# Chunk attention: a mask tile for the far scores, a joint maximum by a seeded minimum, one exponential a block, reciprocals once a step

## The chip, the cores and the metric

The kernel runs on one core of a Trainium2 chip. The metric is the device time of one execution in microseconds (us). Engines: PE is TensorE (matrix products and transposes), DVE is VectorE, ACT is ScalarE, POOL is GpSimd, and SP issues most of the DMAs. Each engine works through its own list of instructions in order, and semaphores make it wait for the others.

## The reference, cut to what matters

A trunk of two layers over 1024 positions of width 1024. The first is a mixer of two recurrent kinds, the second is softmax attention over chunks of 64 positions; each is followed by an MLP and a gated embedding. The change lies in the attention alone:

```python
q = rmsnorm(qkv[:, :, 0], q_g) * (C_HEAD_DIM ** -0.5)      # 16 heads of 64
k = rmsnorm(qkv[:, :, 1], k_g)
rel = jnp.arange(CHUNK)[:, None] + pad - jnp.arange(band)[None, :]   # pad = 8*64, band = 9*64
bias = rel_bias[:, jnp.clip(rel, -C_MAX_REL, C_MAX_REL) + C_MAX_REL]  # C_MAX_REL = 256
...
s = jnp.einsum('bqhd,bkhd->bhqk', q_c, k_b) + bias
s = jnp.where(valid, s, -jnp.inf)
prob = jax.nn.softmax(s, -1)
return jnp.einsum('bhqk,bkhd->bqhd', prob, v_b)
```

Each chunk of 64 queries sees its own chunk and the eight before it. The bias of a head is one constant for all distances from 256 up, and softmax doesn't change when a constant is taken from a whole row: so the kernel takes that constant off, and the far keys need no bias at all.

## The kernel before, in words

The second layer's attention works in 16 steps: 8 pairs of heads, and for each pair two halves of 512 positions. `attn_in` makes q, k and v of a half-step by matrix products (tile `dps` in the profile, from the weights `wq`), `attn_norm` transposes q and k (`dps<-ident,qk`) and scales them into `F` and `Ql`, `attn_block` does the attention, and `attn_sums` scales and stores the result of a finished step.

A block is one head and one tile of 128 queries, numbered m = 0 to 7 over the sequence; there are 16 x 8 = 128 blocks. Its key tiles fall in two groups. The near ones (up to 3 tiles of 128 keys: m-2, m-1, m) get a bias tile `toep`, which also masks. The far ones (up to 2: m-4 and m-3) get none, only a corner that is masked. Blocks with m of 0 to 2 have no far tile (48 blocks), m of 3 has one (16 blocks), m of 4 to 7 have two (64 blocks). For each block:

- PE makes the near scores in the PSUM tile `sn` (two buffers) and the far scores in `sf` (one buffer).
- DVE adds the bias to the near scores, writes them to `pb` and takes their maximum (L2024, an operation and the read of its accumulator). For the far ones it writes the masked corner into `sf` (L2031), takes their maximum (L2032) and forms the negated joint maximum in `mx` (L2033; without far keys L2036).
- ACT takes the exponential of the far scores from `sf` (L2034) and of the near ones in `pb` (L2037), each with the sum of its row.
- DVE adds the two sums (L2039) and takes the reciprocal into `rl` (L2041). In the last two steps ACT also scales `pb` by it (L2043).

Two blocks make a job. PE transposes `pb` into `pt` (two PSUM buffers), ACT and DVE split it into two parts in `ptile` (L352 a rounded copy, L353 the remainder), and PE multiplies it with the values into `po`. Two lanes of jobs run beside each other, with the projections of a later step as filling for PE. At the end of each of the first 14 steps `attn_sums` transposes the eight columns of `rl` on PE, stores them, loads them back as rows, and POOL scales the result.

The order of the work comes from two places: `run` takes the next piece from the lanes by planned times, with the delays of a table, and the tile framework's scheduler then puts the instructions of each engine in order by its own estimates. So an edit in `attn_block` can also move instructions around it.

Of the kernel before, what the change touches and what calls it, by code (L numbers as in the profile page):

```python
# [8 lines left out]
F32 = mybir.dt.float32  # L9
F32R = mybir.dt.float32r  # L10
I32 = mybir.dt.int32
AF = mybir.ActivationFunctionType
ALU = mybir.AluOpType
AX = mybir.AxisListType
# [3 lines left out]
P = 128  # L18
# [3 lines left out]
HB = 512  # L22
NT = T // P
C = 128
NEG = -1.0e30
# [87 lines left out]
class Trunk:  # L113
# [393 lines left out]
    def layer0_in(self):  # L507
        nc, tc, a = self.nc, self.tc, self.a
        with ExitStack() as es:
# [15 lines left out]
            self.halo = {}  # L525
            self.S = {}
            for key in ["la", "lg"] + [f"r{p}{j}" for p in range(4) for j in range(3)]:
                self.halo[key] = l0.tile([P, 1], F32, tag="h_" + key, name="h_" + key)
            for n in range(4):
                for j in range(3):  # L530
                    self.halo[f"g{n}{j}"] = l0.tile([P, 3], F32, tag=f"h_g{n}{j}", name=f"h_g{n}{j}")
                self.S[f"r{n}"] = l0.tile([P, 64], F32, tag=f"Sr{n}", name=f"Sr{n}")
                self.S[f"g{n}"] = l0.tile([P, P], F32, tag=f"Sg{n}", name=f"Sg{n}")
            for t in list(self.halo.values()) + list(self.S.values()):
                nc.gpsimd.memset(t, 0.0)
# [389 lines left out]
    def rwkv_back(self, p, hf, sc, st, u):  # L925
# [31 lines left out]
        Btm, Ktm = tm  # L957
        S = self.S[f"r{p}"]
        py = psm.tile([P, HB], F32, tag="y", name="py")

        for c in range(4):

            Sh = h2.tile([P, 2, 64], F32, tag="Sh", name="Sh", bufs=2)
            V.scalar_tensor_tensor(Sh, S.rearrange("p (o i) -> p o i", o=1).broadcast_to((P, 2, 64)), ee[:, c:c + 1],
                                   self.blk.rearrange("p (h i) -> p h i", h=2), op0=ALU.mult, op1=ALU.mult)
# [805 lines left out]
    def layer1_in(self):  # L1771
        nc, tc, a = self.nc, self.tc, self.a
        with ExitStack() as es:
            self.psm = es.enter_context(self.pool("psml1", space=PSUM))
            wp = self.wp = es.enter_context(self.pool("l1a", 2))
            self.wr = es.enter_context(self.pool("l1wr", 2))
            self.w1 = es.enter_context(self.pool("l1w1"))
            l1 = es.enter_context(self.pool("l1", 2))
            self.sm = es.enter_context(self.pool("sml1", 2))
            self.yd = [[self.dr.tile([P, HB], F32, tag=f"yd{k}{hf}", name="yd") for hf in range(2)] for k in range(NK)]  # L1780
            rbl = l1.tile([P, 16], F32, tag="rbl", name="rbl", bufs=1)
            nc.sync.dma_start(out=rbl, in_=a["rb_last"].rearrange("(o c) -> o c", o=1).broadcast_to((P, 16)))

            steps = [(pr, hf) for pr in range(8) for hf in range(2)]
            self.st = {}

            self.ql = [[pool.tile([P, HB], F32R, tag=tag, name="Ql", bufs=1) for pool, tag in
                        ((self.accp, f"acc{e}"), (l1, f"Ql{e}"))] for e in range(2)]
            jobs = iter([(s, h, b) for s in range(16) for h in range(2) for b in range(2)])
            self.run([self.attn_lane(steps, jobs, l1, rbl) for _ in range(2)] + [self.attn_sums(steps, l1)] + [self.attn_norms(steps, l1), self.attn_ins(steps, l1)])  # L1790
# [55 lines left out]
    def attn_sums(self, steps, l1):  # L1846

        nc = self.nc
        for s, (pr, hf) in enumerate(steps[:14]):
            yield ("at", s)  # L1850
            rd = self.dr.tile([1, T], F32, tag="rd", name="rd", bufs=2)
            pt = self.psm.tile([P, HB], F32, tag="pt", name="pt", bufs=2)[0:8, 0:P]
            self.tr(pt, self.st[s]["rl"].rearrange("p h m -> p (h m)"), self.ident)
            rt = self.sm.tile([8, P], F32, tag="rt", name="rt")
            nc.scalar.copy(rt, pt)
            yield "attn_sums0"
            nc.sync.dma_start(out=rd.rearrange("o (m q) -> (o m) q", m=8), in_=rt)
            yield "attn_sums1"
            R, y = l1.tile([P, HB], F32, tag="R", name="R", bufs=1), self.st[s]["y"]
            for h in range(2):  # L1860
                nc.sync.dma_start(out=R[64 * h:64 * h + 64], in_=rd[:, h * HB:h * HB + HB].broadcast_to((64, HB)))
            yield "attn_sums2"
            nc.gpsimd.tensor_tensor(y, y, R, op=ALU.mult)
            nc.sync.dma_start(out=self.yd[pr][hf], in_=y)
        yield ("at", 14)
        self.mark(("sums", 14))
# [105 lines left out]
    def attn_block(self, s, pr, hf, h, blk, l1, rbl):  # L1972

        nc, psm, sm = self.nc, self.psm, self.sm
        V, A, G = nc.vector, nc.scalar, nc.gpsimd
        st = self.st[s]
        m0 = 4 * hf + 2 * blk
        if hf == 0 and blk == 0:
            t = st["toep"][h]
# [3 lines left out]
        Q, Ql, K, vs, toep = st["Q"], st["Ql"], st["K"], st["vs"], st["toep"][h]  # L1983

        def score(ps, m, j0, n):
            qs = slice((m % 4) * P, (m % 4) * P + P)
            o = 0
            while o < n:
                j = j0 + o
                e = min(n - o, 4 - j % 4)  # L1990
                ks = slice((j % 4) * P, (j % 4 + e) * P)
                k = K[j // 4]
                self.mm(ps[:, o * P:(o + e) * P], Q[:, h, qs], k[:, h, ks], start=True, stop=False)
                self.mm(ps[:, o * P:(o + e) * P], Ql[h][:, qs], k[:, h, ks], start=False, stop=True)
                o += e
# [18 lines left out]
        for m in (m0, m0 + 1):  # L2014
            n0 = max(0, m - 2)
            nn = m - n0 + 1
            f0 = max(0, m - 4)
            nf = n0 - f0
            pn = psm.tile([P, HB], F32, tag="sn", name="sn", bufs=2)
            score(pn[:, 0:nn * P], m, n0, nn)  # L2020
            mx = sm.tile([P, 4], F32, tag="mx", name="mx", bufs=4)
            pb = self.wp.tile([P, 5 * P], F32, tag="pb", name="pb", bufs=4)
            S = pb[:, nf * P:(nf + nn) * P]
            V.tensor_tensor_reduce(S, pn[:, 0:nn * P], toep[:, (3 - nn) * P:], op0=ALU.add, op1=ALU.max,  # L2024
                                   scale=1.0, scalar=NEG, accum_out=mx[:, 0:1])
            l = sm.tile([P, 4], F32, tag="l", name="l", bufs=4)
            if nf:
                pf = psm.tile([P, HB], F32, tag="sf", name="sf")
                score(pf[:, 0:nf * P], m, f0, nf)
                if m >= 4:  # L2030
                    V.memset(pf[64:128, 0:64], NEG)  # L2031
                V.reduce_max(mx[:, 1:2], pf[:, 0:nf * P], axis=AX.X)  # L2032
                V.tensor_scalar(mx[:, 2:3], mx[:, 0:1], mx[:, 1:2], -1.0, op0=ALU.max, op1=ALU.mult)  # L2033
                A.activation(pb[:, 0:nf * P], pf[:, 0:nf * P], AF.Exp, bias=mx[:, 2:3], accum_out=l[:, 1:2])  # L2034
            else:
                V.tensor_scalar(mx[:, 2:3], mx[:, 0:1], -1.0, None, op0=ALU.mult)  # L2036
            A.activation(S, S, AF.Exp, bias=mx[:, 2:3], accum_out=l[:, 0:1])  # L2037
            if nf:
                V.tensor_tensor(l[:, 0:1], l[:, 0:1], l[:, 1:2], op=ALU.add)  # L2039
            rl = st["rl"][:, h, m % 4:m % 4 + 1]  # L2040
            V.reciprocal(rl, l[:, 0:1])  # L2041
            if s > 13:
                A.activation(pb[:, 0:(nf + nn) * P], pb[:, 0:(nf + nn) * P], AF.Copy, scale=rl)  # L2043
            probs.append((pb, f0))
            yield "attn_block0"
        yield "attn_block1"
# [8 lines left out]
        for b in range(bank + 1):  # L2055
            pt = psm.tile([P, HB], F32, tag="pt", name="pt", bufs=2)
            for j, (bb, o, c0, c1) in place.items():
                if bb != b:
                    continue
                for e in range(2):  # L2060
                    if c0 <= 128 * e < c1:
                        pb, f0 = probs[e]
                        self.tr(pt[:, o + 128 * e - c0:o + 128 * e - c0 + P],
                                            pb[:, (j - f0) * P:(j - f0 + 1) * P], self.ident)
            t = self.wp.tile([P, 2, HB], F32R, tag="ptile", name="ptile", bufs=3)
# [120 lines left out]
```

## Time and profile before

| what | value |
|---|---|
| median of 3 runs (lowest to highest) | 3078.52 us (3070.69 to 3079.13) |
| the profiled execution: its time, its span | 3086.63 us, 3084.8 us |
| PE busy, share of the span | 2970.1 us, 96% |
| DVE, ACT, POOL busy | 2209.9 us (72%), 1486.2 us (48%), 552.9 us (18%) |
| attention stage (about 1690 to 2300 us of the span): matrix products and transposes on PE there | 3456 |
| granted clock of PE over the span | 0.974 of full speed |

The page's busy share is a mean over stages with different limits. A table of stretches of the span gives busy time by engine and the granted clock of each stretch; the list of waits of PE says which engine it stood still for; the groups by line give the time of one instruction. The attention stage is the one the diff touches; the other stages hold the same instructions in the same order in both kernels.

### The profile page before, as it was taken

How to read it: one execution, taken by the hardware profiler on the slowest of the kernel's cores; microseconds unless marked ns; L12 is line 12 of the kernel's file. 1: busy time of each engine (PE TensorE's matmuls, PEld its weight loads, DVE VectorE, ACT ScalarE, POOL GpSimd, SP SyncE). 2: the span in 40 equal slices, each digit the busy share in tenths (PEclk: the TensorE clock that was granted, in tenths of full speed). 3: DMA queues.
4: the chain of work that ended last, by engine and by line, in shares of the span. 5: the costliest groups of instructions: out<-in, count | busy, mean ns of one | idle time of the engine just before them, and what ended most of it. 6: DMA issues, size and time to landing. Idle time of an engine off the chain costs nothing.

```text
span 3084.8 us, 47290 instructions
## 1 busy us (share of the span) xinstructions
PE 2970.1 (96%) x17254; PEld 2457.1 (80%) x17254; DVE 2209.9 (72%) x4546; ACT 1486.2 (48%) x2957; POOL 552.9 (18%) x985
## 2 busy tenths in 40 slices
PE   8999999999999999999999999999999999999999
PEld 6777777777777888788887988898878888888887
DVE  7556766667758777788887676676768777788883
ACT  4333433434437555544444465565757555544441
POOL 5434442443500000000005111111210000000002
PEclk9899999999999999999999999999999999999999
DMA  4212112212346444754424211110256444654433
GB/s 145 64 55 62 54 49 75 61 55 68 110 157 227 162 150 151 262 166 151 151 95 131 70 44 40 43 61 23 75 181 223 163 154 153 237 190 150 150 103 116
DMA packets 194857, 368.49 MB, mean 119 GB/s; under 512 B 46800, under 2 KB 49088, under 8 KB 194624
## 3 DMA queue, kind: packets, MB, share of 16 engines
q1 hardware_dynamic: 163808, 309.35, 31.4%
q10 hardware_dynamic: 30816, 56.11, 4.7%
q8 instruction: 136, 2.23, 0.3%
q14 instruction: 97, 0.79, 0.1%
HBM read 268.86 MB, written 96.53 MB: 118 GB/s over the span
## 4 chain that ended last, share of the span: by engine, by line
PE 71%; DVE 14%; DMA 6%; ACT 4%; issue 2%; POOL 1%; SPq 0%; ACTq 0%; DVEq 0%; POOLq 0%
PE dps L180 57%; PE ch L180 2%; PE po L180 2%; DVE act L1283 2%; PE pm L180 1%; PE iz L180 1%; PE pt L195 1%; DMA late<-in_w 1%; PE sn L180 1%; PE tp L180 1%; DMA late<-hd 1%; DVE late L1431 1%; DMA wraw<-in_w_out 1%; PE py L180 1%; DVE wlo L307 1%
## 5 line engine op out<-in xcount | busy, mean ns | idle before, releaser
L180 PE MATMUL dps<-r,act 128*128 128x512 f32 x3720 | 872.9, 392 | 2.0 <-DVE xw L1550 0.8
L180 PEld LDWEIGHTS dps<-r,act 128*128 128x128 f32 x3720 | 698.0, 188 | 157.0 <-issue 1.2
L180 PE MATMUL dps<-xg,whi 128*128 128x512 f32 x1280 | 436.0, 421 | 11.2 <-ACT whi L306 7.4
L1647 POOL TENSOR_TENSOR pn<-pn,prs 128x512 f32<-128x512 f32 x32 | 47.3, 1483 | 1542.6 <-ACT prs L389 1419.5
L180 PE MATMUL dps<-wq,act 128*128 128x384 f32 x1536 | 307.8, 347 | 13.8 <-DVE vs L1909 6.0
L180 PEld LDWEIGHTS dps<-xg,whi 128*128 128x128 f32 x1280 | 236.2, 197 | 62.2 <-ACT whi L306 7.6
L180 PEld LDWEIGHTS dps<-wq,act 128*128 128x128 f32 x1536 | 269.6, 193 | 17.7 <-DVE vs L1909 7.6
L180 PE MATMUL dps<-xg,wlo 128*128 128x512 f32 x640 | 260.7, 407 | 2.6 <-DVE wlo L307 2.6
L1282 ACT CAST act<-act 128x512 fp32r<-128x512 f32 (+2 forms) x281 | 159.3, 600 | 142.0 <-PE dps L180 59.8
L1283 DVE TENSOR_TENSOR act<-act 128x512 fp32r<-128x512 f32 (+2 forms) x281 | 180.1, 669 | 4.6 <-ACT act L1282 4.6
L180 PE MATMUL dps<-act 128*128 128x512 f32 x720 | 176.5, 393 | 2.0 <-DVE late L1404 2.0
L1282 ACT CAST act<-late 128x512 fp32r<-128x512 f32 x210 | 123.7, 620 | 100.4 <-PE dps L180 73.8
L180 PE MATMUL dps<-late,act 128*128 128x512 f32 x672 | 166.6, 392 | 0.0
L180 PEld LDWEIGHTS dps<-act 128*128 128x128 f32 x720 | 136.2, 189 | 32.1 <-DVE late L1404 2.4
L1283 DVE TENSOR_TENSOR act<-late,act 128x512 fp32r<-128x512 f32 x210 | 139.1, 687 | 31.1 <-ACT act L1282 30.9
L180 PEld LDWEIGHTS dps<-xg,wlo 128*128 128x128 f32 x640 | 125.0, 195 | 32.5 <-DVE wlo L307 3.8
L180 PEld LDWEIGHTS dps<-late,act 128*128 128x128 f32 x672 | 126.0, 188 | 27.7
L180 PE MATMUL dps<-xw,act 128*128 128x512 f32 x576 | 145.9, 392 | 0.2 <-ACT act L1282 0.2
L1550 DVE TENSOR_TENSOR xw<-xw,dps 128x512 f32<-128x512 f32 x192 | 130.0, 682 | 17.3 <-PE dps L180 17.2
L306 ACT CAST whi<-wraw 128x1024 fp32r<-128x1024 f32 (+1 forms) x79 | 81.8, 1035 | 107.6 <-PE dps L180 77.1
L180 PEld LDWEIGHTS dps<-xw,act 128*128 128x128 f32 x576 | 107.9, 188 | 24.4 <-ACT act L1282 0.7
L180 PE MATMUL po<-ptile,vs 128*128 128x256 f32 (+1 forms) x576 | 106.8, 295 | 15.5 <-ACT ptile L352 9.7
(488 smaller groups left out, 5600.7 us busy)
## 6 DMA issues: line engine op xcount, KB each, us to landing
hb<-late ACTq DMA_DIRECT2D x196, 256.0 KB
act<-hb SPq DMA_DIRECT2D x158, 256.0 KB
late<-in_w SPq DMA_DIRECT2D x60, 512.0 KB
act<-in_w SPq DMA_DIRECT2D x112, 256.0 KB
wraw<-in_w_in SPq DMA_DIRECT2D x55, 512.0 KB
braw<-hb SPq DMA_DIRECT2D x80, 256.0 KB
wraw<-in_w_out SPq DMA_DIRECT2D x21, 512.0 KB
wraw<-in_w_qkv SPq DMA_DIRECT2D x21, 512.0 KB
```

The costliest lines, as they stand in the source:

```text
L180: return self.begin(self.nc.tensor.matmul(out, lhsT, rhs, start=start, stop=stop, skip_group_check=again))
L195: return self.begin(self.nc.tensor.transpose(out, in_, ident))
L306: nc.scalar.copy(hi, raw)
L307: nc.vector.tensor_tensor(lo, raw, hi.bitcast(F32), op=ALU.subtract)
L1282: A.copy(hi, s)
L1283: V.tensor_tensor(lo, s, hi.bitcast(F32), op=ALU.subtract)
L1431: V.tensor_tensor(t, u, v, op=ALU.subtract)
L1550: V.tensor_tensor(x[n][:, hs[hf]], x[n][:, hs[hf]], ps, op=ALU.add)
L1647: G.tensor_tensor(pn, pn, prs[:, sl], op=ALU.mult)
```

## The change

- A constant tile `far` (128 x 256) is made once on POOL: zeros, with the masked corner of -1e30. Far scores now go through the same DVE operation as near ones, with `far` in place of the bias (the slice that it takes leaves the corner out where there is only one far tile and no mask is wanted in it). Both write to neighbouring columns of `pb`.
- That operation now writes the negated sum (scale -1) and keeps a running minimum. The near one starts from the far one's minimum, so that its result is the joint one, already negated: `tensor_scalar` for it, the maximum over `sf` and the write into `sf` are gone.
- One exponential covers far and near columns (scale -1 turns the sign again), with one sum of the row, which goes straight into `rl`. The addition of the two sums is gone.
- The reciprocal is taken in `attn_sums` of all eight columns at once; only the last two steps still take one a block.
- Far scores now come before near ones on PE.

```diff
+            self.far = l1.tile([P, 2 * P], F32, tag="far", name="far", bufs=1)
+            nc.gpsimd.memset(self.far, 0.0)
+            nc.gpsimd.memset(self.far[64:128, 0:64], NEG)
...
-            self.tr(pt, self.st[s]["rl"].rearrange("p h m -> p (h m)"), self.ident)
+            rl = self.st[s]["rl"].rearrange("p h m -> p (h m)")
+            nc.vector.reciprocal(rl, rl)
+            self.tr(pt, rl, self.ident)
...
-            pn = psm.tile([P, HB], F32, tag="sn", name="sn", bufs=2)
-            score(pn[:, 0:nn * P], m, n0, nn)
-            mx = sm.tile([P, 4], F32, tag="mx", name="mx", bufs=4)
+            mx = sm.tile([P, 2], F32, tag="mx", name="mx", bufs=4)
             pb = self.wp.tile([P, 5 * P], F32, tag="pb", name="pb", bufs=4)
-            S = pb[:, nf * P:(nf + nn) * P]
-            V.tensor_tensor_reduce(S, pn[:, 0:nn * P], toep[:, (3 - nn) * P:], op0=ALU.add, op1=ALU.max,
-                                   scale=1.0, scalar=NEG, accum_out=mx[:, 0:1])
-            l = sm.tile([P, 4], F32, tag="l", name="l", bufs=4)
+            S = pb[:, 0:(nf + nn) * P]
+
+            def biased(ps, j0, n, t, i):
+                score(ps[:, 0:n * P], m, j0, n)
+                V.tensor_tensor_reduce(pb[:, (j0 - f0) * P:(j0 - f0 + n) * P], ps[:, 0:n * P], t, op0=ALU.add, op1=ALU.min,
+                                       scale=-1.0, scalar=mx[:, 0:1] if i else -NEG, accum_out=mx[:, i:i + 1])
             if nf:
-                pf = psm.tile([P, HB], F32, tag="sf", name="sf")
-                score(pf[:, 0:nf * P], m, f0, nf)
-                if m >= 4:
-                    V.memset(pf[64:128, 0:64], NEG)
-                V.reduce_max(mx[:, 1:2], pf[:, 0:nf * P], axis=AX.X)
-                V.tensor_scalar(mx[:, 2:3], mx[:, 0:1], mx[:, 1:2], -1.0, op0=ALU.max, op1=ALU.mult)
-                A.activation(pb[:, 0:nf * P], pf[:, 0:nf * P], AF.Exp, bias=mx[:, 2:3], accum_out=l[:, 1:2])
-            else:
-                V.tensor_scalar(mx[:, 2:3], mx[:, 0:1], -1.0, None, op0=ALU.mult)
-            A.activation(S, S, AF.Exp, bias=mx[:, 2:3], accum_out=l[:, 0:1])
-            if nf:
-                V.tensor_tensor(l[:, 0:1], l[:, 0:1], l[:, 1:2], op=ALU.add)
-            rl = st["rl"][:, h, m % 4:m % 4 + 1]
-            V.reciprocal(rl, l[:, 0:1])
+                biased(psm.tile([P, HB], F32, tag="sf", name="sf"), f0, nf, self.far[:, (2 - nf) * P:], 0)
+            biased(psm.tile([P, HB], F32, tag="sn", name="sn", bufs=2), n0, nn, toep[:, (3 - nn) * P:], 1 if nf else 0)
+            l = st["rl"][:, h, m % 4:m % 4 + 1]
+            A.activation(S, S, AF.Exp, bias=mx[:, 1:2] if nf else mx[:, 0:1], scale=-1.0, accum_out=l)
             if s > 13:
-                A.activation(pb[:, 0:(nf + nn) * P], pb[:, 0:(nf + nn) * P], AF.Copy, scale=rl)
+                V.reciprocal(l, l)
+                A.activation(S, S, AF.Copy, scale=l)
```

In the changed file the lines have other numbers: the biased operation is L2031, the one exponential L2037, the reciprocal of a step L1858.

The edit also moves instructions, by the scheduler's estimates, on all engines. PE has the same products and transposes in both kernels, in another order. On PE at the end of step 1, the second of the first head pair, ahead of the transpose of that step's sums (`pt<-ident,rl`), the kernel before has this (F, Ql: the scaled q and k; the names in front say which tile a product fills):

```order
L180 MATMUL sn<-F_16844,Ql 128x384
L180 MATMUL sn<-F_16844,F_16863 128x384
L180 MATMUL sn<-F_16844,Ql 128x384
L180 MATMUL po<-ptile,vs 128x128 x3
L195 MATMUL pt<-ident,pb 128x128 x4
L180 MATMUL sf<-F_16844,F_16863 128x128
L180 MATMUL sf<-F_16844,Ql 128x128
L195 MATMUL pt<-ident,pb 128x128 x3
L180 MATMUL po<-ptile,vs 128x256
L195 MATMUL pt<-ident,pb 128x128 x2
L180 MATMUL po<-ptile,vs 128x256 x7
L195 MATMUL pt<-ident,rl 8x128
```

The attention's products follow each other there without any projection between them. On PE at the same place the changed kernel has this:

```order
L180 MATMUL dps<-wq_17011,act 128x384 x2
L180 MATMUL dps<-wq_17012,act 128x384
L180 MATMUL dps<-wq_17011,act 128x384 x2
L180 MATMUL po<-ptile,vs 128x256
L180 MATMUL dps<-wq_17012,act 128x384
L180 MATMUL dps<-wq_17011,act 128x384 x2
L180 MATMUL dps<-wq_17012,act 128x384
L180 MATMUL dps<-wq_17011,act 128x384 x2
L195 MATMUL pt<-ident,pb 128x128 x2
L180 MATMUL po<-ptile,vs 128x256 x7
L195 MATMUL pt<-ident,rl 8x128
```

Products of the projection (`dps<-wq`) now stand between the transposes and the product that needs them (`po`).

On PE where a step's q and k are transposed (here the second half of the fourth head pair), the kernel before has this:

```order
L195 MATMUL dps<-ident,qk 128x128 x8
L180 MATMUL sf<-F_17658,F_18107 128x128
L180 MATMUL sf<-F_17658,Ql 128x128
L180 MATMUL sf<-F_18094,F_18107 128x128
L180 MATMUL sf<-F_18094,Ql 128x128
L195 MATMUL pt<-ident,pb 128x128 x6
L180 MATMUL po<-ptile,vs 128x256
```

The changed kernel has, on PE at the same place:

```order
L195 MATMUL pt<-ident,pb 128x128 x6
L195 MATMUL dps<-ident,qk 128x128 x4
L180 MATMUL sf<-F_17512,F_17934 128x256
L180 MATMUL sf<-F_17512,Ql 128x256
L180 MATMUL po<-ptile,vs 128x256
```

Before, the product followed the transposes at once; now four transposes of q or k and two score products stand between them.

Over the stage, of the 144 `ptile`s, 21 had fewer than eight PE instructions between the last transpose into their `pt` and the first product that reads them; in the changed kernel none has. Runs of seven or more transposes of `pb` without anything between were 3 and are 10.

On DVE at the end of step 1, behind the scaling of that half's q and k, the kernel before has this:

```order
L2039 TENSOR_TENSOR l<-l 128x1
L2031 MEMSET sf 64x64
L353 TENSOR_TENSOR ptile<-pt,ptile 128x256
L2036 TENSOR_SCALAR mx<-mx 128x1
L1939 TENSOR_REDUCE ss_17450<-sq 128x8
L2036 TENSOR_SCALAR mx<-mx 128x1
L2041 RECIPROCAL rl<-l 128x1
L2032 TENSOR_REDUCE mx<-sf 128x1
L2033 TENSOR_SCALAR mx<-mx 128x1
```

The changed kernel has, on DVE around the same scaling (`qk<-qk`):

```order
L2031 ISA pb,mx<-sf,far 128x128
L2031 ISA mx 128x1
L353 TENSOR_TENSOR ptile<-pt,ptile 128x256
L293 SCALAR_TENSOR_TENSOR rsw<-rsw,ss_16990 128x16
L2031 ISA pb,mx<-sn,toep,mx 128x384
L2031 ISA mx 128x1
L294 SCALAR_TENSOR_TENSOR nn_16991<-rsw,nn_16991 128x16
L1948 TENSOR_TENSOR qk<-qk,nn_16991 128x1024
L2031 ISA pb,mx<-sn,toep 128x128
```

The small operations of a block on `l`, `rl` and `mx` are gone; a block is two operations with their accumulator reads, and outside the last two steps nothing that DVE does for it waits for ACT any more.

## The prediction

> **What bounds the kernel now.** I read the page's busy times first, then a table of stretches of the span, then the waits of PE in the stage that the diff touches, then that stage in pieces of 4 us, and last the groups of instructions by line and shape.
>
> The page's first part (busy us, share of the span, number of instructions):
>
> ```profile
> PE 2970.1 (96%) x17254; PEld 2457.1 (80%) x17254; DVE 2209.9 (72%) x4546; ACT 1486.2 (48%) x2957; POOL 552.9 (18%) x985
> ```
>
> PE bounds the kernel, and the change gives PE no instruction less. It can gain only where PE stands still or runs at a lower clock. The stretches (start and end, length, busy us of PE, weight load, DVE, ACT, POOL; granted clock, DMA share, GB/s):
>
> ```profile
> 1000.00:1690.00 690.00, 687.48 (x3019) 564.58 (x3017) 530.38 (x828) 331.40 (x577) 43.67 (x27) 1.00 0.48 159
> 1740.00:2200.00 460.00, 426.47 (x2739) 408.72 (x2738) 331.02 (x1096) 281.09 (x724) 69.38 (x66) 0.96 0.13 41
> 2200.00:2300.00 100.00, 89.06 (x492) 75.15 (x490) 76.87 (x205) 69.90 (x156) 21.36 (x16) 0.97 0.49 166
> ```
>
> The stage ahead has PE idle 2.5 us of 690 at full clock. The attention has it idle 33.5 us of 460 and 10.9 of the next 100, and the clock is 0.04 and 0.03 short. So some 44.5 us of idle time and a clock deficit of 0.04 x 460 + 0.03 x 100 = 21.4 us are all there is to win. What PE waits for from 1740 to 2300 us, and the two largest waits of DVE and ACT on each other (us in total, times, longest):
>
> ```profile
> PE po L180 <- ACT ptile L352: 9.7, 11, 1.8
> PE pt L195 <- ACT pb L2034: 4.2, 4, 1.5
> PE dps L180 <- ACT wq L1810: 3.6, 2, 2.9
> PE pt L195 <- DVE ptile L353: 3.3, 5, 1.4
> PE dps L195 <- DVE vs L1909: 3.2, 5, 0.9
> PE po L180 <- DVE ptile L353: 3.1, 6, 0.7
> PE dps L180 <- DVE F L1967: 3.1, 3, 1.2
> PE dps L180 <- POOL act L1708: 2.2, 1, 2.2
> PE sf L180 <- ACT pb L2034: 1.8, 4, 0.6
> ...
> DVE l L2039 <- ACT pb L2037: 25.6, 32, 1.7
> ...
> ACT pb L2034 <- DVE mx L2033: 45.1, 30, 3.9
> ```
>
> PE waits for blocks that are late: for `ptile`, for the exponentials in `pb`, for the buffers of `pt` and `sf` (9.7 + 4.2 + 3.3 + 3.1 + 1.8 = 22.1 us). The last two rows say why blocks are late: DVE stands 25.6 us before the addition of the two sums until ACT is through, and ACT stands 45.1 us before the far exponential until DVE has the joint maximum. Both lists run in order, so each such wait holds whatever is behind it. One of these places, at the end of step 1, in pieces of 4 us and then in ACT's and PE's instructions:
>
> ```profile
> 1804.00:1808.00 4.00, 3.01 (x23) 2.62 (x21) 3.91 (x15) 0.96 (x4) 1.07 (x1) 1.00 0.16 61
> 1808.00:1812.00 4.00, 2.37 (x12) 1.83 (x13) 2.05 (x7) 2.99 (x10) 0.00 (x0) 0.78 0.00 0
> 1812.00:1816.00 4.00, 4.00 (x22) 3.93 (x20) 2.49 (x14) 3.15 (x11) 0.00 (x0) 0.50 0.01 1
> ...
> 1820.00:1824.00 4.00, 4.00 (x32) 3.93 (x30) 1.55 (x5) 1.80 (x3) 1.14 (x1) 1.00 0.17 66
> ```
>
> ```profile
> 1808.06 0.47 ACT L2034 ACTIVATE pb<-sf,mx 128x256 f32<-128x256 f32 x1 [3.10 <-DVE mx L2033]
> ...
> 1809.13 0.39 ACT L2037 ACTIVATE pb<-pb,mx 128x128 f32<-128x128 f32 x1
> ...
> 1808.68 0.55 PE L195 MATMUL pt<-ident,pb 128*128 128x128 f32 x3 [1.16 <-ACT pb L2034]
> ...
> 1810.62 0.58 PE L180 MATMUL po<-ptile,vs 128*128 128x256 f32 x1 [0.80 <-ACT ptile L352]
> ```
>
> DVE is busy 3.91 of 4 us while ACT has nothing for 3.10 us; a small exponential of another block stands behind the far one. PE then waits 1.16 and 0.80 us, and the clock falls to 0.50 in the piece after. There PE gets 22 products through against 32 at full clock, 10/32 of 4 us, or 1.25 us lost for a deficit of 2.0. At that rate the deficit of 21.4 us costs some 13 us.
>
> **The change, part by part.** The rows by line and shape for DVE, then ACT, then one of POOL, from 1690 to 2300 us (busy us, mean ns of one, idle before):
>
> ```profile
> L2024 DVE CUSTOM_DVE_ANT_0 pb<-sn,toep 128x384 f32<-128x384 f32 x96 | 52.0, 552 | 20.4 <-PE pt L195 15.4 <-PE sn L180 4.3
> L353 DVE TENSOR_TENSOR ptile<-pt,ptile 128x512 fp32r<-128x512 f32 x78 | 51.6, 684 | 5.3 <-ACT ptile L352 4.4
> L2032 DVE TENSOR_REDUCE mx<-sf 128x1 f32<-128x256 f32 x64 | 26.7, 417 | 0.6
> ...
> L2041 DVE RECIPROCAL rl<-l 128x1 f32<-128x1 f32 x128 | 19.9, 159 | 5.6 <-ACT pb L2037 3.7
> ...
> L2033 DVE TENSOR_SCALAR mx<-mx 128x1 f32<-128x1 f32 x80 | 16.6, 208 | 1.0
> L2039 DVE TENSOR_TENSOR l<-l 128x1 f32<-128x1 f32 x80 | 15.1, 189 | 26.8 <-ACT pb L2037 25.6
> ...
> L2024 DVE DVE_READ_ACCUMULATOR2_ANT mx<- 128x1 f32 x128 | 10.5, 82 | 0.0
> ...
> L2031 DVE MEMSET sf<- 64x64 f32 x64 | 7.2, 112 | 24.4 <-PE sf L180 23.3
> ...
> L2024 DVE CUSTOM_DVE_ANT_0 pb<-sn,toep 128x256 f32<-128x256 f32 x16 | 6.7, 416 | 0.7 <-PE sn L180 0.6
> ```
>
> ```profile
> L2037 ACT ACTIVATE pb<-pb,mx 128x384 f32<-128x384 f32 x96 | 58.6, 611 | 1.7 <-DVE mx L2036 1.7
> L352 ACT CAST ptile<-pt 128x512 fp32r<-128x512 f32 x78 | 43.1, 584 | 24.0 <-PE pt L195 23.7
> L2034 ACT ACTIVATE pb<-sf,mx 128x256 f32<-128x256 f32 x64 | 30.5, 476 | 45.2 <-DVE mx L2033 44.6
> ...
> L2034 ACT ACTIVATION_READ_ACCUMULATOR pb<-sf,mx 128x1 f32 x80 | 15.8, 198 | 0.0
> ...
> L2043 ACT ACTIVATE pb<-pb,rl 128x640 f32<-128x640 f32 x8 | 6.6, 831 | 2.0 <-DVE rl L2041 1.0 <-DVE rsw L293 1.0
> ```
>
> ```profile
> L1962 POOL MEMSET Ql<- 64x512 f32 x4 | 2.0, 520 | 0.4 <-PE st L180 0.3
> ```
>
> - DVE, a block with two far tiles. Out go the corner 112, the maximum 417, the joint one 208, the addition 189 and the reciprocal 159 ns, 1085 together. In comes the same operation as for two near tiles, 416 + 82. That saves 587 ns, times 64 is 37.6 us. The 16 blocks with one far tile save no more than that each (9.4), the 48 without far keys a reciprocal each (7.6): 38 to 55 us of DVE's 408 in the two stretches. None of it is on PE's path by itself, since DVE has 27% of that time free; it counts where DVE is full, as at 1804.
> - ACT. Out goes 476 + 198 ns of the far exponential; the near one grows from 384 to 640 columns. No exponential of 640 is in this trace. The nearest row is the scaled copy of that width, 831 against 611: 220 ns more. Saved: 454 ns x 64 = 29 us.
> - The chain of a block. From the last score product to the last exponential's end the old way, the near operation being done, takes 112 + 417 + 208 + 476 + 611 = 1824 ns; the new way, the far operation being done, 552 + 82 + 831 = 1465. If both tiles come at once it is 552 + 82 more against 416 + 82 more. It is shorter either way, by 0.36 to 0.50 us.
> - New waits. The near operation stands behind the far one's minimum on DVE, its own list, 82 ns after it. Behind it queue the next subtraction for `ptile` and the norm. The addition, which held DVE 25.6 us for ACT, has no successor, and the reciprocal of a step comes once. It stands in front of a transpose on PE that waited for the last block's reciprocal before; 14 of them at 159 to 208 ns (nearest small rows) are under 3 us of DVE, hidden in its free time, and at most that on PE if the cover is gone.
> - `sf` comes free after 416 ns of DVE instead of after ACT's far exponential; its row among the waits is 1.8 us, at most that is won.
> - POOL writes `far` once, two instructions beside rows of 520 ns: a microsecond at most, ahead of the first block with far keys, hidden behind the first projections. The far corner written into PSUM 64 times goes.
> - No DMA is added or removed; the DMA share is 0.13 here, and I price the moved ones at nothing. If a weight load came late, the bound is the row for `wq` L1810, 3.6 us.
> - The order. Before, 21 of the 144 `ptile`s had fewer than eight PE instructions ahead of their first product, and now none. A split takes 584 + 684 = 1268 ns, and PE spends 426.47/2739 = 156 ns an instruction, so it needs about eight as cover. This hits the largest wait of PE.
>
> The sum. Of the 22.1 us for blocks I take two thirds off, as the short covers go and both queues shorten, but the transposes still stand behind exponentials: 14.7. Of the waits of norm and projection on DVE (3.2 + 3.1) a quarter: 1.6. The 5.8 us for weights and statistics (3.6 + 2.2) stay. Of the remaining 10.3 us a third: 3.4. With about half of the stalls the clock's loss halves: 6.5. Together 26 us. The bounds: all of 22.1 + 6.3 + 10.3 + 13 is 52; nothing is 0; below nothing is the second rival.
>
> Whether the 6.5 us of clock come with the waits is the one term that a rule puts in question. The row: the clock was 0.50 right behind waits of 1.16 and 0.80 us. The rule, in the Trainium skill's page "TensorE: Matmul & The Clock Gate", Part 1: PE's clock halves after at least one idle window of about 3.4 us. By it the waits of this stage would cost no clock, and the change would win 20 us instead of 26; the trace doesn't agree.
>
> **The rivals.**
> - Nothing comes of it. The stalls move: the casts for `ptile` still stand in ACT's list behind exponentials, now of 831 ns instead of 476 and 611 apart, and PE waits elsewhere for as long. For it speaks that the order is an estimate's. Against it: both engines have 29 us and more less to do, and two waits of 25.6 and 45.1 us lose their cause. The time would be 3070 to 3086, about 3078.
> - Slower, by bunched transposes. Runs of seven or more transposes fill both `pt` buffers at once; there were 3, now there are 10. The next transpose then waits for a whole split, 1.27 us, and the clock drops behind it, 1.25 us and more. Seven more such places at 2.5 us are 18 us, so 3096 if nothing else improves. It decides where less than 18 us of the old stalls go. PE's wait for `pt` buffers, 3.3 us with 3 runs, is small, which speaks against it.
> - Waits won, but no clock. If the clock falls here for another reason than these short waits (the longest of the rows is 2.9 us), the change wins 14.7 + 1.6 + 3.4, some 20 us: 3058. The pieces from 1804 to 1816 us, where the fall follows the waits, speak against it. The rule of the Trainium skill's "TensorE: Matmul & The Clock Gate" above would have it so.
>
> **How the numbers follow.** Against the profiled execution (3086.63 us, a span of 3084.8 and 1.8 around it) the sum gives 3060.6. The median of the runs is 3078.52, 8 us lower, so I set the same difference against the median: 3052.5, say 3053. Chances: forecast 0.64 (its own range 3028 to 3067), no clock 0.10, nothing 0.13, bunched transposes 0.13. The range from 3030 to 3082 leaves out the slower rival and the edge of the others. A measurement of this kernel can tell about 0.3% from no change, 9 us. The forecast, except for 0.02 at its weak end, and the case without the clock lie beyond it: faster 0.72, same 0.15, slower 0.13.
>
> **What would show it.** DVE's wait for the addition (25.6) is gone and ACT's wait for DVE before an exponential is well under 45; PE's rows for `po` and `pt` together fall from some 20 us to under 9; PE's idle time from 1740 to 2300 falls from 44.5 to about 25, and the clock in it reaches 0.98; DVE is busy some 50 us less and ACT some 30. I am wrong if PE's idle time stays while DVE's and ACT's busy time falls, or if the far operation, from PSUM with `far`, costs more than 416 ns, or if waits for `pt` buffers grow beyond 15 us.

## The result, and the profile after

The changed kernel takes 3023.38 us (median of 4 runs, 3021.18 to 3027.3) against 3074.74 us of the kernel before on the same chip (4 runs, 3070.69 to 3079.13). The ratio is 0.9832, with a 95% interval of 0.9814 to 0.9849: 51 us or 1.7% faster. The forecast was 25 us, and the time lies below its range. The profiled execution of the kernel before took 3086.63 us, 12 above that median.

The first part of the page after (busy us, share of the span, number of instructions):

```profile
span 3020.1 us, 46853 instructions
...
PE 2932.7 (97%) x17254; PEld 2431.6 (81%) x17254; DVE 2174.3 (72%) x4256; ACT 1467.6 (49%) x2797; POOL 546.5 (18%) x987
```

The two profiled executions are 64.7 us apart, more than the medians. Landmarks in them say where that arises. The first projection of the attention starts at 1685.6 us before and at 1677.7 after, so 7.9 us had gone where both kernels are the same; that is the difference of two executions and no effect of the change (over all kernels here with the scheduler it starts between 1674.2 and 1689.5 us). From the first product of the stage that follows (`dps<-act,late`) to the start of the last product there are 748.5 and 746.0 us. The stage between gives the rest. I cut it so that it holds the same products, from 54.6 us behind the first projection to that landmark. Of before:

```profile
1740.20:2330.60 590.40, 546.02 (x3368) 509.06 (x3369) 421.49 (x1317) 362.88 (x895) 90.74 (x82) 0.97 0.22 71
```

Of after:

```profile
1732.30:2268.10 535.80, 520.49 (x3369) 491.91 (x3368) 385.77 (x1026) 343.09 (x733) 85.70 (x82) 1.00 0.24 77
```

The columns are start and end, length, then busy us of PE, weight load, DVE, ACT and POOL, the granted clock, DMA share and GB/s. 590.4 became 535.8 us, 54.6 less. PE's idle time fell from 44.4 to 15.3, which is 29.1. PE's busy time fell by 25.5 with the same products: they ran faster. Cut into pieces of 4 us, the clock was short in 18 pieces before, by 20.4 us in all (one minus the clock, times the length; I call this the deficit), and in none after. In the trace of before, 150 products of the stage start while the clock is at half; they take 38.2 us, and 20.6 at the mean times that products of the same kinds take in the changed kernel. So some 18 of the 25.5 us lie in the slow clock and some 8 outside it, which no run here explains. The Trainium skill's page "Trainium Kernel Development and Optimization", section Performance Expectations, warns that the busy time of products is a bad metric for how close a kernel is to roofline, since they are pipelined. The trace bears out the warning in its own way: 25.5 us of the gain hide in busy time, most of them through the clock.

What PE waits for after, from 1732 to 2268 us (us in total, times, longest):

```profile
PE pt L195 <- ACT pb L2037: 2.9, 10, 0.3
PE sn L180 <- DVE mx L2031: 2.8, 6, 1.0
PE pt L195 <- DVE ptile L353: 2.6, 5, 0.9
PE po L180 <- DVE ptile L353: 1.7, 6, 0.4
PE dps L180 <- ACT sq L1706: 1.7, 2, 1.5
PE dps L195 <- DVE F L1973: 0.7, 3, 0.3
PE po L180 <- DVE y L2082: 0.7, 1, 0.7
PE po L180 <- ACT ptile L352: 0.6, 1, 0.6
PE dps L180 <- POOL act L1708: 0.3, 1, 0.3
```

The wait of `po` for ACT's part of `ptile` went from 9.7 to 0.6 us, the one for exponentials from 4.2 and more to 2.9 in short pieces. The largest wait of ACT for DVE is still there after, from 1690 to 2300 us:

```profile
ACT pb L2037 <- DVE mx L2031: 41.7, 33, 3.4
```

It was 45.1. So the hold of ACT by DVE (the time that ACT stands waiting for DVE) did not go away, while PE's waits for ACT shrank.

The groups by line and shape after, DVE and then ACT (busy us, mean ns, idle before):

```profile
L2031 DVE CUSTOM_DVE_ANT_0 pb<-sn,toep,mx 128x384 f32<-128x384 f32 x80 | 49.0, 612 | 2.5 <-PE sn L180 0.7
L2031 DVE CUSTOM_DVE_ANT_0 pb<-sf,far 128x256 f32<-128x256 f32 x64 | 26.9, 420 | 25.1 <-PE sf L180 23.8 <-PE pt L195 1.0
...
L2031 DVE CUSTOM_DVE_ANT_0 pb<-sn,toep 128x384 f32<-128x384 f32 x16 | 8.9, 555 | 2.2 <-PE pt L195 2.1
...
L1858 DVE RECIPROCAL rl<-rl 128x8 f32<-128x8 f32 x14 | 2.8, 197 | 1.3 <-ACT pb L2037 1.0
```

```profile
L2037 ACT ACTIVATE pb<-pb,mx 128x640 f32<-128x640 f32 x64 | 53.3, 832 | 38.0 <-DVE mx L2031 37.6
```

The far operation takes 420 ns, as taken from its twin (416), and the exponential of 640 takes 832 (831). The near operation with a seed takes 612, without one 555.

### The profile page after: what moved, and what is told of

Same layout as the page of the kernel before. It is cut to its first block, busy times and chain, and to the rows that moved or that the text cites. A ratio compares the mean times of both kernels' runs of the same rounds, so it can differ in the third digit from the quotient of the medians.

```text
span 3020.1 us, 46853 instructions
## 1 busy us (share of the span) xinstructions
PE 2932.7 (97%) x17254; PEld 2431.6 (81%) x17254; DVE 2174.3 (72%) x4256; ACT 1467.6 (49%) x2797; POOL 546.5 (18%) x987
## 4 chain that ended last, share of the span: by engine, by line
PE 78%; DVE 11%; DMA 4%; ACT 3%; issue 2%; POOL 2%; SPq 0%; ACTq 0%; DVEq 0%; POOLq 0%
PE dps L180 64%; PE ch L180 2%; PE po L180 2%; PE pm L180 1%; PE pt L195 1%; PE iz L180 1%; PE sn L180 1%; PE tp L180 1%; DMA wraw<-in_w_out 1%; DVE wlo L307 1%; PE py L180 1%; DVE act L1283 1%; DVE pb L2031 1%; POOL sub L420 1%; DMA late<-in_w 1%
## 5 line engine op out<-in xcount | busy, mean ns | idle before, releaser
L180 PEld LDWEIGHTS dps<-late,act 128*128 128x128 f32 x672 | 126.0, 188 | 27.7
L307 DVE TENSOR_TENSOR wlo<-wraw,whi 128x1024 fp32r<-128x1024 f32 (+1 forms) x79 | 101.6, 1287 | 15.3 <-ACT whi L306 14.9
```

The source lines that it names most:

```text
L180: return self.begin(self.nc.tensor.matmul(out, lhsT, rhs, start=start, stop=stop, skip_group_check=again))
L307: nc.vector.tensor_tensor(lo, raw, hi.bitcast(F32), op=ALU.subtract)
```

## The experiments

Two theories stood at first. The queues: DVE and ACT have less to do and hold each other less, so blocks are ready earlier. The order: the scheduler, with another picture of the chains, puts the instructions in a better order, and on the chip it is that order which counts. A third came up with the first results.

All times are medians in us. The ratios are to the kernel before, run beside each kernel on the same chip; its median there was 3074.74 to 3078.84. Idle, busy and clock deficit are those of the stage cut as above, in one profiled execution. "Short covers" counts, in the built order, the `ptile`s with fewer than eight PE instructions between the last transpose and the first product that reads them, of 144.

| kernel | time | ratio to before (95%) | PE idle | PE busy | deficit | short covers |
|---|---|---|---|---|---|---|
| before | 3074.74 | 1 | 44.4 | 546.0 | 20.4 | 21 |
| the change | 3023.38 | 0.9832 (0.9814 to 0.9849) | 15.3 | 520.5 | 0.0 | 0 |
| before, emitted order | 3141.91 | 1.0212 (1.0175 to 1.0249) | 43.0 | 542.6 | 6.8 | 9 |
| change, emitted order | 3133.52 | 1.0189 (1.0158 to 1.0219) | 39.3 | 536.2 | 3.4 | 3 |
| change with DVE ballast | 3035.90 | 0.9876 (0.9840 to 0.9912) | 19.0 | 528.0 | 0.0 | 0 |
| change, two exponentials | 3026.66 | 0.9839 (0.9808 to 0.9869) | 17.1 | 525.4 | 3.4 | 1 |
| before, far scores copied | 3039.47 | 0.9878 (0.9857 to 0.9900) | 23.5 | 522.7 | 1.7 | 2 |
| the same, `sf` held | 3066.55 | 0.9968 (0.9951 to 0.9984) | 38.1 | 542.8 | 20.4 | 16 |
| change, two exponentials, `sf` held | 3047.08 | 0.9895 (0.9871 to 0.9919) | 27.7 | 534.2 | 10.2 | 12 |
| before, reciprocal of a step | 3077.59 | 1.0006 (0.9994 to 1.0018) | 46.4 | 543.6 | 13.6 | 21 |
| before, ring of three | 3028.67 | 0.9850 (0.9825 to 0.9876) | 18.9 | 523.2 | 3.4 | 1 |
| change, ring of three | 3025.29 | 0.9832 (0.9813 to 0.9851) | 14.9 | 524.7 | 3.4 | 0 |
| change, ring, longer wait | 3023.39 | 0.9822 (0.9804 to 0.9840) | 16.9 | 516.3 | 0.0 | 0 |
| before, ring, emitted order | 3145.43 | 1.0216 (1.0188 to 1.0245) | 44.9 | 542.5 | 8.5 | 3 |

"Emitted order" means without the scheduler, as the lanes wrote the instructions. Two limits of the table: the stage holds 3360 to 3377 products in the kernels with the scheduler, but 3399 with the ballast and some 3340 in the emitted orders; and the profiled execution of the change with two exponentials and `sf` held took 3061.94 us, 15 above its median.

### Without the scheduler

```diff
-    with tile.TileContext(nc, schedule_with_timeline_sim=True) as tc:
+    with tile.TileContext(nc, schedule_with_timeline_sim=False) as tc:
```

> The kernel before, without the framework's scheduler: every engine takes its instructions as the lanes wrote them. Compared with its twin, the changed kernel without the scheduler. First theory (the queues: DVE and ACT have less to do and hold each other less, whatever the order): the twin is faster by 35 us or more. Second theory (the order: the scheduler, seeing shorter chains, put more products between a block's transposes and what reads them): the twin's gain is under 17 us. By itself this one should be slower than the kernel before by 1 to 5%, 3105 to 3230 us; no theory rests on that.

> The changed kernel without the scheduler. Queues: 35 us or more below its twin, with PE's waits for exponentials and for ptile smaller by half. Order: within 17 us of its twin.

In the order in which the lanes wrote them, the change brings 8 us, and the intervals of the two overlap, so no difference is shown. The change's work is the same as with the scheduler: fewer operations, a shorter chain, no addition that waits for ACT. All that, by itself, moved the time little. PE's waits for `ptile` and `pb` did not halve, they went from 17.8 to 14.2 us (two rows of `pb` after, 1.1 and 0.2, are not shown). Of the kernel before without the scheduler, then of the changed one, from 1680 to 2420 us:

```profile
PE pt L195 <- DVE ptile L353: 9.8, 9, 2.0
...
PE po L180 <- DVE ptile L353: 3.3, 7, 0.7
PE sf L180 <- ACT pb L2034: 2.8, 7, 0.7
...
PE po L180 <- ACT ptile L352: 2.4, 3, 1.6
PE pt L195 <- ACT pb L2043: 2.3, 1, 2.3
```

```profile
PE pt L195 <- DVE ptile L353: 7.5, 10, 1.4
...
PE po L180 <- DVE ptile L353: 4.2, 8, 0.8
PE sf L180 <- DVE mx L2031: 3.8, 9, 0.9
...
PE po L180 <- ACT ptile L352: 1.2, 2, 0.6
```

This speaks for the order and against the queues. The stage itself takes no longer in the emitted orders (585.6 and 575.5 us against the 590.4 of before); what they lose, they lose ahead of it, as the first projection starts at 1739.8 and 1743.3 us. So in this stage the scheduler's order of the kernel before was no better than the one as written. The short covers also fell here, from 9 to 3, without a gain, so that count is a mark of a good order and not its cause alone.

### The work given back, and the hold given back

```diff
+            if nf:
+                bal = sm.tile([P, 2 * P], F32, tag="bal", name="bal", bufs=1)
+                V.tensor_tensor(bal, self.far, self.far, op=ALU.add)
+                V.memset(bal[:, 0:64], 0.0)
```

> The changed kernel with DVE work given back: for each of the 80 blocks with far keys an addition over 256 columns and a small write into a tile that nobody reads, about 0.5 us together, some 42 us in all, which waits for nothing. If the amount of DVE's work is what counts, 20 us or more of the 51 come back (3043 us and up). If it is the waits of DVE and ACT for each other, under 10 us come back (below 3033). If the order: what the scheduler makes of it, with fewer products as cover where it is slower.

It took 3035.90 us, some 12 more than the change, between what the two theories of the work and of the waits had. But the ballast did not go into the blocks. It waits for nothing but the tile `far`, and the scheduler put all 80 pairs at the start (ns as lowest, median and highest, then first and last start):

```profile
L2039 DVE TENSOR_TENSOR bal<-far x80: 407/425/1292, 1686.7 to 1797.7; 128x256 f32<-128x256 f32 x80
L2040 DVE MEMSET bal<- x80: 112/112/112, 1687.7 to 1799.8; 128x64 f32 x80
```

They take 45.5 us of DVE there, which is busy 57.2 of the 60 us from 1740 to 1800 against 44.5 in the change, and nothing is added in the rest of the stage. So this run prices a crowd at the start of the stage. What the same work would cost if it were spread over the blocks, it doesn't show.

```diff
-            A.activation(S, S, AF.Exp, bias=mx[:, 1:2] if nf else mx[:, 0:1], scale=-1.0, accum_out=l)
+            nb = mx[:, 1:2] if nf else mx[:, 0:1]
+            if nf:
+                l2 = sm.tile([P, 2], F32, tag="l2", name="l2", bufs=4)
+                A.activation(pb[:, 0:nf * P], pb[:, 0:nf * P], AF.Exp, bias=nb, scale=-1.0, accum_out=l2[:, 1:2])
+            N = pb[:, nf * P:(nf + nn) * P]
+            A.activation(N, N, AF.Exp, bias=nb, scale=-1.0, accum_out=l2[:, 0:1] if nf else l)
+            if nf:
+                V.tensor_tensor(l, l2[:, 0:1], l2[:, 1:2], op=ALU.add)
```

> The changed kernel with the exponential in two parts again (far and near, with a row sum each) and the addition of the sums on DVE, which waits for ACT again. ACT gets some 29 us of work back, DVE 15. If the hold of DVE by ACT counts, 20 us or more come back (3043 and up) and DVE's wait for the addition is above 15 us again. If the amount of work or the operation with the mask tile counts, under 10 us come back.

The time is 3026.66 us, and the intervals of its ratio and the change's overlap almost wholly. Yet DVE waits for ACT as before, from 1680 to 2400 us:

```profile
DVE rl L2044 <- ACT pb L2042: 27.2, 35, 1.3
```

So 27.2 us of hold cost nothing that can be measured. This wait, 25.6 us in the kernel before, was the first reason of my prediction. One exponential in place of two is worth nothing measurable either: in the stage ACT is busy 364.1 us again (343.1 in the change, 362.9 before) and DVE 13 us more than in the change. Here the work does come back block by block.

### What is left: the buffer of the far scores

In the change, and with two exponentials too, DVE copies the far scores out of `sf`, the only PSUM buffer they have. In the kernel before, ACT's far exponential read `sf`, behind the joint maximum. So the third theory was the buffer: held that long, it keeps the scheduler from placing the next far scores, and the order bunches up around it.

The masked operation alone, on the kernel before (with the tile `far` made as in the change):

```diff
-                if m >= 4:
-                    V.memset(pf[64:128, 0:64], NEG)
-                V.reduce_max(mx[:, 1:2], pf[:, 0:nf * P], axis=AX.X)
+                V.tensor_tensor_reduce(pb[:, 0:nf * P], pf[:, 0:nf * P], self.far[:, (2 - nf) * P:], op0=ALU.add, op1=ALU.max,
+                                       scale=1.0, scalar=NEG, accum_out=mx[:, 1:2])
...
-                A.activation(pb[:, 0:nf * P], pf[:, 0:nf * P], AF.Exp, bias=mx[:, 2:3], accum_out=l[:, 1:2])
+                A.activation(pb[:, 0:nf * P], pb[:, 0:nf * P], AF.Exp, bias=mx[:, 2:3], accum_out=l[:, 1:2])
```

> The kernel before with one edit: the far scores go through DVE's masked operation into pb, and the far exponential reads pb. The maximum, the joint one, the two exponentials, the addition on DVE and a reciprocal a block stay, near scores first. So sf, the one PSUM buffer of the far scores, comes free with DVE's operation and not with ACT's exponential. Theory of the buffer: this alone lets the scheduler put the work apart; 3020 to 3045 us. Rival (shorter chains by the joint minimum and fewer small operations): none of those is in here, so within 15 us of the kernel before, 3060 us or more.

The same with `sf` held: the corner is written into `sf` as before, the masked operation runs as above, and the far exponential reads `pf` again.

```diff
+                if m >= 4:
+                    V.memset(pf[64:128, 0:64], NEG)
...
-                A.activation(pb[:, 0:nf * P], pb[:, 0:nf * P], AF.Exp, bias=mx[:, 2:3], accum_out=l[:, 1:2])
+                A.activation(pb[:, 0:nf * P], pf[:, 0:nf * P], AF.Exp, bias=mx[:, 2:3], accum_out=l[:, 1:2])
```

> As the one before, with the masked operation, but the far exponential reads sf again (and DVE writes the corner into sf for it), so the copy in pb is overwritten and sf is held until ACT is through. Theory of the buffer: the gain is gone, 3060 to 3095 us. Rival (the masked operation is better for DVE than the maximum): below 3045.

3039.47 and 3066.55 us: 37 and 9 us below the kernel before. The two differ in what the exponential reads and in a write of 112 ns, and 27 us lie between them. The stage with the scores copied, then with `sf` held:

```profile
1730.70:2276.90 546.20, 522.66 (x3360) 490.59 (x3359) 411.85 (x1321) 364.62 (x892) 86.06 (x82) 1.00 0.23 75
```

```profile
1734.50:2315.40 580.90, 542.79 (x3362) 507.63 (x3361) 419.03 (x1386) 362.13 (x892) 91.93 (x82) 0.96 0.22 71
```

ACT and DVE are as busy in both, within 8 us. PE's idle time and the clock falls are back with the hold.

Held in the change, with two exponentials:

```diff
-                biased(psm.tile([P, HB], F32, tag="sf", name="sf"), f0, nf, self.far[:, (2 - nf) * P:], 0)
+                pf = psm.tile([P, HB], F32, tag="sf", name="sf")
+                biased(pf, f0, nf, self.far[:, (2 - nf) * P:], 0)
+                if m >= 4:
+                    V.memset(pf[64:128, 0:64], NEG)
...
-                A.activation(pb[:, 0:nf * P], pb[:, 0:nf * P], AF.Exp, bias=nb, scale=-1.0, accum_out=l2[:, 1:2])
+                A.activation(pb[:, 0:nf * P], pf[:, 0:nf * P], AF.Exp, bias=nb, accum_out=l2[:, 1:2])
```

> The changed kernel with two exponentials, of which the far one reads sf, with the corner written into it: sf is held until ACT is through; the joint minimum, the far scores first and the reciprocal of a step stay as in the change. Theory of the buffer: slower than with two exponentials out of pb (3026.7 us) by 25 us or more, 3052 to 3090. Rival (the joint minimum and the fewer operations): within 12 us of it, below 3039.

3047.08 us, 20 more than with two exponentials out of `pb`. The theory had 25 or more, its rival 12 or less: it lies between, nearer to the buffer. With the hold back 29 us of the gain stay, where the held copy kept 9. What makes this difference of 20 us is not isolated; the joint minimum and the far scores ahead of the near ones, which this kernel has and the held copy has not, may shorten the hold too, and neither was tried alone.

The reciprocals alone:

```diff
-            rl = st["rl"][:, h, m % 4:m % 4 + 1]
-            V.reciprocal(rl, l[:, 0:1])
             if s > 13:
+                V.reciprocal(rl, rl)
```

Here the sum of a row goes straight into `rl`, and `attn_sums` takes the reciprocals of a step, as in the change.

> The kernel before with the reciprocals once a step, nothing else: 20 us less work on DVE. Theory of the buffer: no gain, within 10 us of the kernel before. Theory of the queues: 10 to 20 us faster.

3077.59 us, a ratio of 1.0006 (0.9994 to 1.0018). It shows no effect. DVE's busy time in the stage fell by 7 us only (421.5 to 414.3), not by the expected 20, so the run says little of a larger saving.

### The buffer without the change

```diff
-            pn = psm.tile([P, HB], F32, tag="sn", name="sn", bufs=2)
+            pn = psm.tile([P, HB], F32, tag="sn", name="sn", bufs=3)
...
-                pf = psm.tile([P, HB], F32, tag="sf", name="sf")
+                pf = psm.tile([P, HB], F32, tag="sn", name="sf", bufs=3)
```

The third user of `sn`, a projection at the start of the stage, has three buffers as well.

> The kernel before, with nothing of the change: only the three PSUM buffers of the scores (two of sn, one of sf) are made one ring of three that near and far scores take in turn. DVE and ACT have all their old work, and the far exponential still reads PSUM. Theory of the buffer: most of the change's gain without the change, 3020 to 3045 us, and clock falls nearly gone. Rival (what the operations cost and how they hold each other): within 12 us of the kernel before, 3063 us or more.

3028.67 us, a ratio of 0.9850 (0.9825 to 0.9876). No operation of DVE or ACT is gone, and nearly the whole gain is there. The stage of this kernel, then the waits of DVE and of ACT for each other in it:

```profile
1728.80:2270.90 542.10, 523.22 (x3369) 494.13 (x3368) 420.58 (x1316) 360.62 (x893) 83.47 (x82) 0.99 0.23 77
```

```profile
DVE l L2039 <- ACT pb L2037: 17.6, 38, 1.3
```

```profile
ACT pb L2034 <- DVE mx L2033: 35.5, 30, 3.4
```

DVE is busy 420.58 us, as before the change (421.49), and both holds are still there. PE's idle time is 18.9 us instead of 44.4, its busy time 523.2 instead of 546.0. So no operation has to go for the gain; with the scheduler, a free score buffer is enough. The ring frees near and far scores alike, the change frees `sf` alone. That letting go of `sf` is one way to the gain, the two pairs with and without the hold show, with 27 us on the kernel before and 20 on the changed one. How the rest of the change's 51 us comes about is not isolated.

The same ring, by the same edits, on the changed kernel, and then with one number of the planner's table raised:

> The changed kernel with the same ring of three. Theory of the buffer: the hold is gone in the change already, so little is left: 3010 to 3027 us, within 13 us of the changed kernel. Rival (the buffers bound it still): below 3005.

```diff
-    "attn_block2": 0.43,
+    "attn_block2": 0.80,
```

> The same, with one number of the planner's table raised (the wait after a transposed block from 0.43 to 0.80), which puts more products between transposes and what reads them. If cover on PE is what is left of the waits, 5 us or more below the one before; if the rest of the waits is on other things, within 5 us of it.

3025.29 and 3023.39 us. The hold was gone in the change already, and more cover for `ptile` brings nothing that can be measured, so no version here beats the changed kernel.

Last, the ring without the scheduler, both edits shown above together:

> The kernel before with the ring of three score buffers and without the scheduler, so that the order of the lanes stays as written. If the free buffer gains through the scheduler's order, little is won here: within 13 us of the same without the ring (3141.9 us). If the buffer is what the chip itself waits for, whatever the order, 30 us or more are won (below 3112).

3145.43 us, against 3141.91 without the ring: nothing is won. In the emitted order the same free buffer is worth nothing; it gains where the scheduler can use it to move instructions. So it is not enough that the chip has the buffer. No run takes the work of one kernel in the order of the other, so that the order alone makes the gain is argued from these runs together, and not shown by a single one.

## Why the prediction went wrong, point by point

- That PE bounds, and that it can win only idle time and clock, was right for most of it. Idle time and busy time, 29.1 and 25.5 us, are the whole 54.6 of the stage; some 8 us of the busy time lie outside the slow clock, and the prediction had no term for them.
- The waits for blocks were sized right: 22.1 us, two thirds off, made 14.7; the rows for `po`, `pt` and `sf` after, without that of `y`, add up to 8.2 (the two smallest, 0.2 each, are not shown above), so 13.9 went. In part that was luck. Of the reasons given, the short covers did go, from 21 to none, but the two holds that should lose their cause, 25.6 and 45.1 us, were wrong: the first can be given back for nothing, and the second is still 41.7 after.
- The step that failed is the bullet on `sf`: "its row among the waits is 1.8 us, at most that is won". A row of waits says what a buffer costs in the order that was built around it. It can't say what another order costs. Free score buffers, by the ring alone, were worth 50 us; holding `sf` or not made 20 to 27. A second step failed beside it, the clock's term, below.
- The order as such was seen, but as one help among several. Without the scheduler the change is worth 8 us, not clear of its noise.
- The waits that I let stand (5.8 us, for weights and statistics) shrank to 0.3, and those of norm and projection on DVE went from 6.3 to 0.7 where a quarter was taken. That is some 9.5 us of the error. I put both down to the same order; no run isolates them.
- The clock was mis-sized: 6.5 us forecast, and some 18 came in the two profiled executions. I let the falls halve with the stalls, but all of them went. My price for a us of deficit, 0.62, comes from counts of products in two pieces that hold different products; 18 us for 20.4 of deficit is 0.9. Another measure is nearer to mine: over 39 further executions of the kernel before, the time grows by 0.58 us for each us of deficit over the whole span (a straight line, correlation 0.89), and then 20.4 us are worth 12. (Over the eleven kernels with the scheduler in the table the busy time grows by 1.2 us for each us of deficit, but these differ in their order too.) Two of the 39 have a clock of 0.985 over the span, as the change has in its two fastest executions. They took 3063.33 and 3063.77 us, the change 3021.18 and 3022.12: some 42 us of the gain are there without a difference in the clock over the span. So the slow clock is the smaller part, 12 to 18 us by these two measures.
- DVE's saving (38 to 55 us) came out at 35.7, partly since the near operation costs 60 ns more with a seed. ACT's 29 us were 19.8: I added the read of the accumulator as if it stood alone, while in the trace the next exponential starts 0.47 us behind the far one (1808.53 after 1808.06, in a row that my fence leaves out), as long as the far one takes: the read is hidden. By the runs with two exponentials and with the ring, neither mattered for the time.
- Rivals: bunched transposes didn't bite, since the wait for `pt` buffers went from 3.3 to 2.6. The case without the clock was wrong in the other direction. The sum's own bound, all the idle time but 5.8 us and all of the clock's 13, was 52 us, and nearly that came, with other parts: 29.1 us of idle time and 25.5 of busy time. The range stopped short of it at 3030.

## What to carry to other kernels

Where a scheduler makes the order, look for the buffer with one copy and ask who reads it last: an operation that copies it out early, or a ring that it shares with its neighbours, can change the order of a whole stage, and the row of waits for that buffer won't show it. Price a stall of PE as idle time plus the slow clock behind it. Here the slow clock went wholly or nearly so (0 to 3.4 us of deficit) in every kernel with the scheduler whose idle time in the stage came below 24 us. Before you read an experiment that adds work, look in the trace where the scheduler put it. To learn whether operations or their order are worth the time, run both kernels once without the scheduler.

## What was unexpected of the hardware

The clock's deficits in the stage are whole multiples of 1.7 us in every kernel here that has any: 1.7, 3.4, 6.8, 8.5, 10.2, 13.6 and 20.4. A fall lasts some 3.4 us or a whole multiple of it, at half clock: the one behind the waits of 1.16 and 0.80 us runs from about 1810.2 to 1817.1 us, twice as long. That is the length of the window that the Trainium skill's page "TensorE: Matmul & The Clock Gate", Part 1, gives, at its half rate, and there trace and page agree. What starts a fall differs: by the page an idle window does. In the kernel before the stage has eight falls, and in the 3.4 us ahead of each PE stood idle for only 1.2 to 2.1 us; here the measurement decides. Other stretches of 3.4 us with up to 1.8 us of idle time had no fall behind them, so what decides is open. In the changed kernel the longest single wait of the stage was 1.5 us, and the clock didn't fall.

DVE's operation with a minimum that is seeded from memory took 612 ns for 384 columns against 555 with a constant. It is the same operation otherwise, in the same kernel; what of the 57 ns is the operand and what is its wait was not tried apart.
